# One list of projections for both mixers, dealt out in other shares

## The chip, the cores and the metric

The kernel runs on one core of a Trainium2 chip. Its engines work side by side, each through its own queue in order: TensorE (PE) multiplies matrices, VectorE (DVE), ScalarE (ACT) and GpSimd (POOL) do the elementwise work, and SyncE (SP) issues the DMAs. The metric is the device time of one launch in microseconds (us), lower is better. Loading of a weight into PE is shown as PEld; it can run beside a matmul.

## What is computed

One encoder block on 1024 tokens of width 1024, in float32. An input projection gives everything that two mixers need; a bidirectional gated linear attention (GLA, 4 heads) and a windowed attention with keys shared by groups of heads (8 heads, 2 key heads, blocks of 128, windows of three blocks) run on it; their outputs are gated, merged and projected, and a SwiGLU feed-forward follows.

```python
h = _rms_norm(x, norm_mix_g[l])
proj = h @ w_in[l]
(g_q, g_k, g_v, g_r, g_lr_f, g_lr_b,
 s_q, s_k, s_v, gate_a, gate_b) = jnp.split(proj, split_at, axis=-1)
y_gla = _gla_branch(g_q, g_k, g_v, g_r, ...) @ w_o_gla[l]
y_swa = _swa_branch(s_q, s_k, s_v, ...) @ w_o_swa[l]
merged = jax.nn.sigmoid(gate_a) * y_gla + jax.nn.sigmoid(gate_b) * y_swa
x = x + merged @ w_out[l]
h2 = _rms_norm(x, norm_ffn_g[l])
gu = h2 @ w_ffn_in[l]
ff_gate, ff_up = gu[..., :D_FF], gu[..., D_FF:]
x = x + (jax.nn.silu(ff_gate) * ff_up) @ w_ffn_out[l]
```

In GLA, each head goes through chunks with a state that is carried forward, and once more backward; here a chunk is 128 tokens, so there are 8 chunks a head and 32 in all. The output of a head is normalized per token and multiplied by silu(r). In the attention, queries and keys are normalized and rotated, and a learned logit per head joins the softmax.

## The kernel before

**Precision.** Every float32 matrix product is done in three matmuls in a reduced float32 form: an operand is split into a high part (ACT copies it) and a remainder (POOL or DVE subtracts), and high x high, high x low and low x high add up. A weight unit is a tile of 128x512 (256 KB) that `wunit` (L61 to L68) loads on SP's queue, copies on ACT (`wh`, L65) and subtracts on POOL (`wl`, L67).

**Projections as fillers.** The input projection is cut into named pieces that run as generators, one matmul a step. `proj_f(name, m)` (L161) makes a 128x1024 piece with the features on the partitions: 2 units, 48 matmuls, and then two tiles that DVE scales by the norm (L147) and SP stores to a scratch in DRAM. `proj_t(name, n)` (L180) makes a 1024x512 piece with the tokens on the partitions: 16 units, 192 matmuls, and eight tiles that ACT scales (L208) and SP stores (L209). `next_unit` (L156) takes the weight units in the order in which the pieces were made, up to three ahead. All pieces wait in the list `dense` (L213). `fill(n)` (L215) runs n steps of it, `need(key)` (L224) runs it until a stored piece is there, and `slot(stages, n)` (L228) calls the given stages one after the other and spreads n steps between them.

**GLA.** 32 chunks go through six stages: `g_gates`, `g_sums`, `g_scores`, `g_out`, and in the order of the backward pass `g_back_out` and `g_turn`. The loop at L474 deals them out to slots: chunk n has its gates in slot n, its sums in n + 1, its scores in n + 2, its output in n + 3; the backward output is in slot cb (L468), and the turn, which transposes the normalized output and stores it, one slot later. In a slot the latest stage comes first (the turn, then the backward output, the output, scores, sums, gates). From slot 35 on only backward outputs and turns of the last head are left (the drain). `dense` holds at that time v0, q1, k1, q2, k2, v1, q3, k3, skv, sq0 and sq1, and a slot asks for 64, 48 or 20 steps (L475).

**Attention.** After GLA's pools are closed (L478), those of the attention are opened, and their constants are loaded on SP's queue (L484 to L489). Then r0 to r7 and ga0, gb0 to ga7, gb7 join `dense` (L618 to L620). Sixteen pairs of key group and query block run through `k_prep` and `k_turn` (keys: load, norm, rotation, transpose), `a_prep` and `a_turn` (queries), `a_scores` (four heads, and the softmax behind the last of them, ending in the scaling at L588), `a_probs` (transposes of the probabilities, L599) and `a_out`. `todo` (L621) has 22 slots of 70 steps; what is left of `dense` runs at the end (L637).

**The merge.** Its pools are opened when the attention's are closed (L638). For each half of the tokens, 8 tiles of the GLA output are loaded, gated and split (L664 to L678), 8 tiles of the attention output are loaded and split (L679 to L687), and then groups of 24 matmuls multiply them with the output weights (L652, L695), before the output projection and the feed-forward.

**What sets the order.** PE's instructions of the two loops stand under `tc.manual_schedule` (L473, L633), which keeps PE's order as written within each loop. All else, the order on ACT, DVE, POOL and SP included, comes from a scheduler that goes by dependences, priorities and free buffers. In the trace of before, matmuls of the second loop stand between those of the end of the first.

Of the kernel before, what the change touches and what calls it, by code (L numbers as in the profile page):

```python
# [16 lines left out]
KT = 8  # L17
HT = 512
NH = 4
NC = 8  # L20
# [7 lines left out]
def body(tc, i, out):  # L28
    nc = tc.nc
    with ExitStack() as root:  # L30
# [9 lines left out]
        def nm(s):  # L40
            uid[0] += 1
            return f"{s}_{uid[0]}"

        def mmtile(shape=(P, 512), dt=F32):
            return psm.tile(list(shape), dt, tag="mm", name=nm("mm"))
# [4 lines left out]
        def scratch(name, shape=(P, 512)):  # L50
            return dram.tile(list(shape), F32, tag=name, name=name)

        def stage(shape=(P, 512), dt=F32):
            return stg.tile(list(shape), dt, tag="st", name=nm("st"))
# [15 lines left out]
        def mm(o, a, b, start, stop):  # L70
            nc.tensor.matmul(o, a, b, start=start, stop=stop)  # L71
# [67 lines left out]
        def proj_f_out(name, b):  # L139
            for s in range(2):  # L140
                d = scratch(f"{name}_{s}")
                t = stage()
                if name[0] == "q":
                    nc.vector.scalar_tensor_tensor(t, b[s], 128 ** -0.5, rstd[:, s * HT:(s + 1) * HT],
                                                   op0=ALU.mult, op1=ALU.mult)
                else:
                    nc.vector.tensor_tensor(t, b[s], rstd[:, s * HT:(s + 1) * HT], op=ALU.mult)  # L147
                nc.sync.dma_start(out=d, in_=t)
                scr[name, s] = d
# [6 lines left out]
        def next_unit():  # L156
            while plan and len(ready) <= AHEAD:
                ready.append(wunit(plan.pop(0)))
            return ready.pop(0)

        def proj_f(name, m):  # L161
            plan.extend(i["w_f"][m, u] for u in range(2))

            def steps():
                b = [mmtile(), mmtile()]
                for u in range(2):
                    h, l = next_unit()
                    for kk in range(4):
                        k = u * 4 + kk
                        c = slice(kk * P, (kk + 1) * P)  # L170
                        st, sp = k == 0, k == KT - 1
                        for o, w, x, f0, f1 in ((b[0], h, xh[k][0], st, False), (b[0], h, xl[k][0], False, False),
                                                (b[1], h, xh[k][1], st, False), (b[1], h, xl[k][1], False, False),
                                                (b[0], l, xh[k][0], False, sp), (b[1], l, xh[k][1], False, sp)):
                            mm(o, w[:, c], x, f0, f1)
                            yield
                proj_f_out(name, b)
            return steps()

        def proj_t(name, n):  # L180
            for s in range(2):
                plan.extend(i["w_t"][n, k] for k in range(KT))

            def steps():
                for s in range(2):
                    b = [mmtile() for _ in range(4)]
                    us = []

                    def unit_mm(k, t):
                        h, l = us[k]  # L190
                        c = slice(t * P, (t + 1) * P)
                        st, sp = k == 0, k == KT - 1
                        for x, w, f0, f1 in ((xh, h, st, False), (xh, l, False, False), (xl, h, False, sp)):
                            mm(b[t], x[k][s][:, c], w, f0, f1)
                            yield

                    for k in range(KT):
                        us.append(next_unit())
                        if k < KT - 2:
                            for t in range(4):  # L200
                                yield from unit_mm(k, t)
                    for t in range(4):
                        yield from unit_mm(KT - 2, t)
                        yield from unit_mm(KT - 1, t)
                        ti = s * 4 + t
                        d = scratch(f"{name}_{ti}")
                        o = stage()
                        nc.scalar.activation(o, b[t], AF.Copy, scale=rstdt[:, ti:ti + 1])  # L208
                        nc.sync.dma_start(out=d, in_=o)  # L209
                        scr[name, ti] = d  # L210
            return steps()

        dense = []  # L213

        def fill(n):  # L215

            while n > 0 and dense:
                try:
                    next(dense[0])
                    n -= 1  # L220
                except StopIteration:
                    dense.pop(0)

        def need(key):  # L224
            while key not in scr:
                fill(12)

        def slot(stages, n):  # L228

            stages = [f for f in stages if f]  # L230
            done = 0
            for j, f in enumerate(stages):
                f()
                t = n * (j + 1) // len(stages)
                fill(t - done)
                done = t
# [213 lines left out]
        def g_turn(hd, c):  # L450
# [6 lines left out]
            for j in range(2):  # L457
# [1 line left out]

        dense += [proj_t("v0", 0), proj_f("q1", 2), proj_f("k1", 3), proj_f("q2", 4), proj_f("k2", 5),  # L460
                  proj_t("v1", 1), proj_f("q3", 6), proj_f("k3", 7), proj_t("skv", 2), proj_t("sq0", 3),
                  proj_t("sq1", 4)]

        at = {}
        last = 0
        for n in range(NH * NC):
            hd, c = divmod(n, NC)
            cb = hd * NC + NC + 3 + (NC - 1 - c)  # L468
            for j, (t, f) in enumerate(((n, g_gates), (n + 1, g_sums), (n + 2, g_scores), (n + 3, g_out),
                                        (cb, g_back_out), (cb + 1, g_turn))):  # L470
                at[t, j] = (f, hd, c)
                last = max(last, t)
        with tc.manual_schedule(engines={mybir.EngineType.PE}):  # L473
            for t in range(last + 1):  # L474
                n = 64 if t < 4 else 48 if t < NH * NC + 3 else 20  # L475
                slot([(lambda v=at[t, j]: v[0](*v[1:])) if (t, j) in at else None for j in (5, 4, 3, 2, 1, 0)], n)
        need(("sq0", 7))
        glas.close()  # L478


# [42 lines left out]

        def k_prep(t):
            kv = sw.tile([P, 4, P], F32, tag="kvr", name=nm("kvr"), bufs=1)
            nc.sync.dma_start(out=kv.rearrange("p a b -> p (a b)"), in_=scr["skv", t])
            v2 = kv[:, 2:4].rearrange("p a b -> p (a b)")
            nc.scalar.activation(vSh[t], v2, AF.Copy)
            nc.gpsimd.tensor_tensor(vSl[t], v2, vSh[t].bitcast(F32), op=ALU.subtract)
            keys[t] = norm_rope(kv[:, 0:2], 2, t, kg, 1.0 / 128, EPS, epst)  # L530
# [84 lines left out]
                nc.sync.dma_start(out=scr["b", 4 * g + h, n // 4][:, (n % 4) * P:(n % 4 + 1) * P],  # L615
                                  in_=ob[:, h])

        dense += [proj_f(f"r{m}", 8 + m) for m in range(8)]  # L618
        for m in range(8):
            dense += [proj_f(f"ga{m}", 16 + m), proj_f(f"gb{m}", 24 + m)]  # L620
        todo = [[] for _ in range(2 * KT + 6)]  # L621
        for n in range(2 * KT):
            g, t = divmod(n, KT)
            todo[n + 5].append((a_out, g, t))
            todo[n + 4] += [(a_probs, g, t, kb) for kb in range(3)]
            todo[n + 3] += [(a_scores, g, t, h) for h in range(4)]
            todo[n + 2].append((a_turn, g, t))
            todo[n + 1].append((a_prep, g, t))
            if n < KT:
                todo[n + 1].append((k_turn, n))  # L630
                todo[n].append((k_prep, n))
        order = (a_out, a_probs, a_scores, a_turn, k_turn, k_prep, a_prep)
        with tc.manual_schedule(engines={mybir.EngineType.PE}):  # L633
            for t, v in enumerate(todo):
                v.sort(key=lambda e: order.index(e[0]))
                slot([lambda e=e: e[0](*e[1:]) for e in v], 70)
            fill(1 << 30)  # L637
        swas.close()  # L638
        xstack.close()
# [9 lines left out]
        def btile(tag, dt=F32, bufs=None):  # L649
            return bt.tile([P, HT], dt, tag=tag, name=nm(tag), bufs=bufs)  # L650
# [11 lines left out]
        for s in range(2):  # L662
            oa, ob = ([], []), ([], [])
            for k in range(KT):  # L664
                o = btile("lo")
                nc.sync.dma_start(out=o, in_=scr["o", k, s])
                r = btile("lr")
# [195 lines left out]
```

## Time and profile before

| what | us |
|---|---|
| median of the runs (3) | 1959.8 |
| lowest and highest | 1957.63, 1961.05 |
| the profiled execution, its device time | 1960.35 |
| its span in the trace | 1958.6 |
| PE busy in the span | 1829.8 (93%) |
| PEld busy | 1491.0 (76%) |
| DVE, ACT, POOL busy | 828.7, 716.4, 722.6 |
| mean granted clock of PE | 0.967 |

The times in the text are microseconds from the start of the span. A page of the profile shows the span in 40 equal slices, with the busy share of each engine in tenths; the clock in the same form is the share of full speed that PE was granted. A row of the timeline has the start, the duration, the engine, the line, the operation and what it writes and reads ("mm<-xh,wl" is a matmul into a tile mm from xh and wl), and in brackets the idle time before it with what ended it. Many matmuls have the line of a helper, L71, and are told apart by their tiles: xh and xl are the halves of the normed input, so a matmul with one of these is a step of a projection (features first: mm<-xh,wh and its kin; tokens first: mm<-wh,xh), ob with ident is a turn, U is a sum, vr, vh and vl belong to the values, p with ident is a transpose of probabilities, oah, oal and obh, obl are the merge's operands. Matmuls are pipelined: one starts before the one ahead of it has ended, so their durations add up to more than the time that they take.

### The profile page before, as it was taken

The numbers are of one execution on the slowest core, as the hardware profiler recorded it, in microseconds if no ns is written. First come the engines' busy times: TensorE is split into PE (matmuls) and PEld (weight loads), VectorE is DVE, ScalarE is ACT, GpSimd is POOL, SyncE is SP. The second block draws the span as 40 slices with busy tenths as digits, with TensorE's granted clock in tenths as the row PEclk, the third lists the DMA queues.
The fourth block names the chain that finished last, engine by engine and source line by source line (L and its number), as shares of the span: only waits on it lengthen the run. The fifth ranks groups of instructions, "written<-read, shape, count | busy, mean of one in ns | idle before, by whom it ended". The sixth has DMA issues, their size and how long they took to land. (4 is left out here: it accounts for less than half of the span.)

```text
span 1958.6 us, 24074 instructions
## 1 busy us (share of the span) xinstructions
PE 1829.8 (93%) x8340; PEld 1491.0 (76%) x8340; DVE 828.7 (42%) x1783; ACT 716.4 (37%) x1607; POOL 722.6 (37%) x632
## 2 busy tenths in 40 slices
PE   5899999998389999995798999899999999999999
PEld 3688888887268888873587888688888888888887
DVE  7235566669477766554535234221112111221112
ACT  3344566678433433334444334422112211221120
POOL 6344445544043322221455445533223322332231
PEclk9999999999689999996799999999999999999999
DMA  5343444442233323323557444111121112111212
GB/s 156 95 132 100 132 125 130 138 143 76 60 111 108 97 89 95 103 78 116 170 155 214 144 130 124 38 49 41 44 57 49 42 45 60 49 42 45 60 49 87
DMA packets 126665, 184.91 MB, mean 94 GB/s; under 512 B 14574, under 2 KB 50414, under 8 KB 126544
## 3 DMA queue, kind: packets, MB, share of 16 engines
q1 hardware_dynamic: 126544, 183.38, 31.3%
q8 instruction: 66, 1.08, 0.2%
q14 instruction: 55, 0.45, 0.1%
HBM read 143.48 MB, written 39.85 MB: 94 GB/s over the span
## 5 line engine op out<-in xcount | busy, mean ns | idle before, releaser
L67 POOL TENSOR_TENSOR wl<-wr,wh 128x512 fp32r<-128x512 f32 (+1 forms) x386 | 493.9, 1281 | 923.6 <-ACT wh L65 828.6
L65 ACT ACTIVATE wh<-wr 128x512 fp32r<-128x512 f32 (+1 forms) x386 | 237.3, 615 | 726.9 <-PE mm L71 690.6
L71 PE MATMUL mm<-yh,wh 128*128 128x512 f32 x704 | 276.5, 393 | 0.0
L71 PE MATMUL mm<-yl,wh 128*128 128x512 f32 x704 | 276.0, 392 | 0.0
L71 PE MATMUL mm<-xh,wh 128*128 128x512 f32 (+1 forms) x528 | 213.3, 404 | 14.2 <-ACT xh L277 11.5
L71 PE MATMUL mm<-xl,wh 128*128 128x512 f32 (+1 forms) x528 | 214.2, 406 | 10.4 <-DVE xl L278 10.3
L71 PE MATMUL mm<-yh,wl 128*128 128x512 f32 x704 | 220.5, 390 | 0.0
L71 PE MATMUL mm<-xh,wl 128*128 128x512 f32 (+1 forms) x528 | 178.1, 404 | 0.0
L71 PEld LDWEIGHTS mm<-yh,wh 128*128 128x128 f32 x704 | 132.5, 188 | 33.8 <-DVE st L745 6.7
L71 PEld LDWEIGHTS mm<-yh,wl 128*128 128x128 f32 x704 | 132.7, 189 | 28.4 <-issue 0.8
L71 PEld LDWEIGHTS mm<-yl,wh 128*128 128x128 f32 x704 | 132.6, 188 | 27.8 <-issue 0.8
L71 PE MATMUL mm<-fh,wh 128*128 128x512 f32 x352 | 137.5, 391 | 0.0
L71 PE MATMUL mm<-fl,wh 128*128 128x512 f32 x352 | 137.1, 389 | 0.2 <-DVE fl L749 0.2
L745 DVE TENSOR_TENSOR st<-mm,st 128x512 f32<-128x512 f32 x44 | 30.4, 692 | 244.6 <-PE mm L71 216.4
L71 PEld LDWEIGHTS mm<-xl,wh 128*128 128x128 f32 (+1 forms) x528 | 100.6, 191 | 35.9 <-DVE xl L278 15.9
L71 PE MATMUL mm<-wl,xh 128*128 128x512 f32 x320 | 128.0, 400 | 0.0
L71 PE MATMUL mm<-wh,xh 128*128 128x512 f32 x320 | 127.1, 397 | 0.0
L71 PE MATMUL mm<-wh,xl 128*128 128x512 f32 x320 | 127.0, 397 | 0.0
L71 PEld LDWEIGHTS mm<-xh,wh 128*128 128x128 f32 (+1 forms) x528 | 100.6, 191 | 34.7 <-ACT xh L277 11.5
L71 PEld LDWEIGHTS mm<-xh,wl 128*128 128x128 f32 (+1 forms) x528 | 98.5, 191 | 19.0
L71 PE MATMUL mm<-fh,wl 128*128 128x512 f32 x352 | 109.0, 389 | 0.0
L774 DVE TENSOR_TENSOR x<-mm,x 128x512 f32<-128x512 f32 x48 | 30.9, 686 | 152.8 <-PE mm L71 152.8
(218 smaller groups left out, 3343.2 us busy)
## 6 DMA issues: line engine op xcount, KB each, us to landing
wr<-in_w_fi_dram SPq DMA_DIRECT2D x88, 256.0 KB, 2.6
wr<-in_w_t_dram SPq DMA_DIRECT2D x80, 256.0 KB, 2.7
wr<-in_w_f_dram SPq DMA_DIRECT2D x64, 256.0 KB, 2.8
wr<-in_w_fo_dram SPq DMA_DIRECT2D x48, 192.0 KB, 2.3
wr<-in_w_oa_dram SPq DMA_DIRECT2D x32, 256.0 KB, 2.8
wr<-in_w_ob_dram SPq DMA_DIRECT2D x32, 256.0 KB, 2.7
wr<-in_w_out_dram SPq DMA_DIRECT2D x32, 256.0 KB, 2.9
xr<-in_xT_dram SPq DMA_DIRECT2D x16, 256.0 KB, 2.8
```

What stands on the lines that cost most here:

```text
L65: nc.scalar.activation(h, raw, AF.Copy)
L67: nc.gpsimd.tensor_tensor(l, raw, h.bitcast(F32), op=ALU.subtract)
L71: nc.tensor.matmul(o, a, b, start=start, stop=stop)
L745: nc.vector.tensor_tensor(u, bu[s], g, op=ALU.mult)
L774: nc.vector.tensor_tensor(x1[m][s], y[s], x1[m][s], op=ALU.add)
```

## The change

All pieces go into `dense` before GLA starts, in the same order as before: r0 to r7 and the gates stand behind sq1. The steps per slot are 40 in the first six slots of GLA, 31 up to slot 34 and 18 in the drain; 60 in the first two slots of the attention, 46 in the next sixteen and 28 in the rest. The turn of the last head comes two slots behind its backward output instead of one, so that the loop has one more slot. The wait for the last piece of sq0 behind the loop goes, and `k_prep` has one for its piece of skv.

```diff
         dense += [proj_t("v0", 0), proj_f("q1", 2), proj_f("k1", 3), proj_f("q2", 4), proj_f("k2", 5),
                   proj_t("v1", 1), proj_f("q3", 6), proj_f("k3", 7), proj_t("skv", 2), proj_t("sq0", 3),
-                  proj_t("sq1", 4)]
+                  proj_t("sq1", 4)] + [proj_f(f"r{m}", 8 + m) for m in range(8)]
+        for m in range(8):
+            dense += [proj_f(f"ga{m}", 16 + m), proj_f(f"gb{m}", 24 + m)]
...
             for j, (t, f) in enumerate(((n, g_gates), (n + 1, g_sums), (n + 2, g_scores), (n + 3, g_out),
-                                        (cb, g_back_out), (cb + 1, g_turn))):
+                                        (cb, g_back_out), (cb + (2 if hd == NH - 1 else 1), g_turn))):
...
             for t in range(last + 1):
-                n = 64 if t < 4 else 48 if t < NH * NC + 3 else 20
+                n = 40 if t < 6 else 31 if t < NH * NC + 3 else 18
...
-        need(("sq0", 7))
         glas.close()
...
         def k_prep(t):
             kv = sw.tile([P, 4, P], F32, tag="kvr", name=nm("kvr"), bufs=1)
+            need(("skv", t))
...
-        dense += [proj_f(f"r{m}", 8 + m) for m in range(8)]
-        for m in range(8):
-            dense += [proj_f(f"ga{m}", 16 + m), proj_f(f"gb{m}", 24 + m)]
         todo = [[] for _ in range(2 * KT + 6)]
...
-                slot([lambda e=e: e[0](*e[1:]) for e in v], 70)
+                slot([lambda e=e: e[0](*e[1:]) for e in v], 60 if t < 2 else 46 if t < 2 * KT + 2 else 28)
             fill(1 << 30)
```

## The prediction

> **What bounds the kernel now.** I read the page first, its 40 slices above all, then busy time by stretch, then single rows of the timeline.
>
> ```profile
> span 1958.6 us, 24074 instructions
> ...
> PE   5899999998389999995798999899999999999999
> ...
> PEclk9999999999689999996799999999999999999999
> ```
>
> A slice is 49 us. TensorE (PE) is the bound nearly everywhere, except in two holes, around slices 10 to 12 and 19 to 20, where its clock is lower too. The slots of the diff end in both. Busy time by stretch (the columns are the stretch, its length, then busy us with instruction counts of PE, PEld, DVE, ACT and POOL, then granted clock, DMA share, GB/s):
>
> ```profile
> 72.30:432.60 360.30, 360.29 (x1824) 301.64 (x1824) 193.13 (x442) 203.22 (x519) 168.51 (x161) 1.00 0.43 127
> 432.60:545.60 113.00, 65.06 (x369) 52.56 (x368) 82.13 (x277) 71.49 (x247) 27.33 (x33) 0.78 0.25 73
> 545.60:873.00 327.40, 327.37 (x1556) 270.82 (x1557) 213.55 (x601) 117.41 (x302) 95.15 (x98) 0.99 0.32 98
> 873.00:906.00 33.00, 24.55 (x107) 19.17 (x106) 18.91 (x61) 15.12 (x41) 1.29 (x1) 0.84 0.16 48
> 906.00:972.60 66.60, 38.28 (x120) 25.54 (x120) 31.51 (x33) 27.03 (x45) 24.49 (x19) 0.69 0.57 180
> ```
>
> Filled slots leave PE no idle time at all (row 1, row 3); the holes are rows 2, 4 and 5. From 432.6 us the first list of projections is used up: 256 + 20 x 48 = 1216 steps go to slots 0 to 23, the last 32 to slot 24. Then come the drain of the GLA mixer, the start of the attention, and from 873 us the attention without filling and the start of the merge.
>
> To price a hole I need what a matmul costs when nothing waits, and that is its pitch, not its duration:
>
> ```profile
> 263.53 0.38 PE L454 MATMUL ch<-ident,ob 128*128 128x128 f32 x2
> ...
> 269.25 0.39 PE L71 MATMUL mm<-wh,xl 128*128 128x512 f32 x1
> ...
> 270.89 0.39 PE L71 MATMUL mm<-wh,xh 128*128 128x512 f32 x1
> ...
> 277.97 0.38 PE L454 MATMUL ch<-ident,ob 128*128 128x128 f32 x2
> ```
>
> The middle rows are first and last of 8 steps: 1.64 / 7 = 0.234 us a step, though each is shown with 0.39. From turn to turn a GLA slot takes 14.44 us: 48 steps are 11.2, so the 28 small matmuls of six stages take 3.2 us, 0.116 each.
>
> **The change part by part.** A step is one matmul; proj_f has 48, proj_t 192. The list is now: v0, v1, skv, sq0, sq1 give 960, q1 to k3 six times 48 = 288, together 1248; r, ga, gb give 24 x 48 = 1152; 2400 in all. No matmul is added or removed; each fills another place.
>
> GLA slots. 6 x 40 + 29 x 31 + 10 x 18 = 1319 steps (the last turn moves one slot later, so the loop has 45 slots). The list lasts. A full slot becomes 31 x 0.234 + 3.2 = 10.5 us. Does something else become late in it? The tightest chain goes from the sums to the next slot's scores:
>
> ```profile
> 317.42 0.28 PE L71 MATMUL ch<-U,ll 128*128 128x256 f32 x1
> ...
> 321.37 0.78 POOL L359 TENSOR_TENSOR kl<-en,kh 128x256 fp32r<-128x256 f32 x1
> ```
>
> It needs 322.15 - 317.54 = 4.6 us. The new distance is 10.5 less the sums' own 0.5 and the scores' turn before them (0.7 + 5 steps, 1.2): 8.1 us. Room 3.5. Engine load:
>
> ```profile
> 335.86:350.33 14.47, 14.47 (x77) 12.21 (x76) 11.58 (x29) 11.34 (x33) 6.84 (x7) 1.00 0.47 142
> ```
>
> DVE 11.6 and ACT 11.3 us in one of the fullest slots, with four weight units converted in it (31 steps bring 2.6). Even unshrunk they would exceed 10.5 by 1.1, on 29 slots 32 us; with the projections' share removed (ACT: 1.4 units and some 0.8 output tiles fewer) they fit. I take 0, bounds 0 and 32.
>
> First slots. 40 instead of 64 brings g_out(0,0), the first to use v0, closer to v0's first tile:
>
> ```profile
> 92.95 0.69 ACT L208 ACTIVATE st<-mm,rstdt 128x512 f32<-128x512 f32 x1 [0.41 <-PE mm L71]
> ...
> 100.50 0.74 POOL L370 TENSOR_TENSOR vl<-vr,vh 128x256 fp32r<-128x256 f32 x1 [0.49 <-ACT vh L369]
> ```
>
> From copy through DRAM to the split tile 8.3 us; the tile is done at step 79 and read at step 120, 41 x 0.234 = 9.6 us plus 1.2 of stages. It holds by 2.5 us. All later need() keys are done long before (q1, k1 after 288 steps, needed after 302), so need adds nothing; that of skv is met too, and the removed need(sq0) was met already.
>
> Hole 1, row 2. Its 113.0 us hold 369 matmuls. How many of them are steps shows by their moving tiles (xh, then xl, in 433 to 546 us):
>
> ```profile
> 433.00:546.00 113.00, 15.81 (x47) 0.78 0.25 73
> 433.00:546.00 113.00, 9.56 (x24) 0.78 0.25 73
> ```
>
> 71 steps. That is the first attention slot's share (70): it depends on nothing there and was pulled ahead into the gaps of the GLA slots. 71 x 0.234 + 298 x 0.116 = 51.2 us of work, so **61.8 us** are empty or half-speed. Where they lie:
>
> ```profile
> 524.96 0.66 PE L454 MATMUL ch<-ident,ob 128*128 128x128 f32 x2 [2.68 <-DVE ob L448]
> ...
> 528.94 0.66 PE L454 MATMUL ch<-ident,ob 128*128 128x128 f32 x2 [2.68 <-DVE ob L448]
> ...
> 545.63 0.66 PE L535 MATMUL ch<-ident,qn 128*128 128x128 f32 x2 [16.03 <-DVE qn L515]
> 545.94 1.20 PE L71 MATMUL mm<-xh,wl 128*128 128x512 f32 x2
> ...
> 551.59 0.39 PE L71 MATMUL mm<-xh,wh 128*128 128x512 f32 x1
> ```
>
> A drain slot takes 4.0 us, nearly all the chain to ob. Now it holds 18 steps, 4.2 us, and the turn has two slots: the chain (under 4.0) is hidden. Then the first keys: 545.63 - 528.94 = 16.7 us of copying out, constants, load and norm. Over that now lie 18 steps of the last slot and 60 of the first attention slot: 78 x 0.234 = 18.3 us. The cover is 1.6 us longer than the chain, with SP, ACT and POOL also serving weights; I put 1 us here, bounds 0 and 14 (the 60 steps pulled ahead again). The half-speed matmuls after it go: 14 steps in 5.65 us instead of 3.3, **2.4 us**.
>
> Hole 2a, row 4. A filled attention slot gives the small matmuls' pitch:
>
> ```profile
> 817.10:839.40 22.30, 22.30 (x108) 18.53 (x107) 13.35 (x38) 8.39 (x20) 5.28 (x5) 1.00 0.26 83
> ```
>
> 22.3 - 70 x 0.234 = 5.9 us for 38, 0.155 each. 107 x 0.155 = 16.6 of 33.0 us: **16.4 us** go, as the slots now hold 2 x 60 + 16 x 46 + 3 x 28 = 940 steps (the 22nd slot has no stage and fills nothing) of the 1081 left, and 141 remain for the end.
>
> Hole 2b, row 5. 120 x 0.234 = 28.1 of 66.6 us: **38.5 us** empty or slow, while the merge's operands are made:
>
> ```profile
> 905.79 0.49 PE L71 MATMUL ch<-ph,vSl 128*128 128x512 f32 x1
> ...
> 909.95 0.32 SPq L666 DMA_DIRECT2D lo<-o  x1
> ...
> 941.20 1.36 DVE L676 TENSOR_TENSOR oal<-lo,oah 128x512 fp32r<-128x512 f32 x2
> ...
> 961.67 0.69 DVE L685 TENSOR_TENSOR obl<-lo,obh 128x512 fp32r<-128x512 f32 x1 [1.37 <-ACT obh L684]
> ```
>
> After the attention's last matmul the GLA half is ready 36.8 us later, the other half 56.6 us. Over it now lie 28 + 141 = 169 steps, 39.5 us. Some 17 stay, and PE has two groups of 24 matmuls of the GLA half for them, 11.2 us: I leave 6 us, bounds 0 and 17.
>
> What the shorter attention slots cost. A slot is now 46 x 0.234 + 5.9 = 16.7 us. One chain is tight, from the fourth head's scores to the first transpose of probabilities:
>
> ```profile
> 834.26 0.56 DVE L568 CUSTOM_DVE_ANT_0 p<-ch,band 128x384 f32<-128x384 f32 x1 [1.60 <-PE ch L71]
> ...
> 840.27 1.39 DVE L588 TENSOR_SCALAR p<-p,rd 128x384 f32<-128x384 f32 x4
> ...
> 843.12 0.60 PE L599 MATMUL ch<-ident,p 128*128 128x128 f32 x4
> ...
> 880.42 2.56 PE L599 MATMUL ch<-ident,p 128*128 128x128 f32 x12 [3.12 <-DVE p L588]
> ```
>
> It takes 7.4 us (834.26 to 841.66) and waits for nothing now, as the transpose comes 8.9 us on. In the new slots of 10 stages four shares of 4.6 steps and the turn and out matmuls (2.5) lie between: 6.8 us. So PE waits some 0.6 to 1 us in about 8 such slots, less in the five of 12 stages (6 shares of 3.83 steps, 8.0 us), and about 2 in the last two: 10 us. Bounds: 0 (the unfilled slot at 880.42 has a shorter queue before it) and rival 1.
>
> Sum: 61.8 + 2.4 + 16.4 + 38.5 = 119.1 us can go; 1 + 6 + 10 = 17 come back. The profiled execution took 1960.35 us (span 1958.6, 1.75 around it), 0.55 over the runs' median, which is nothing beside this: 1960.35 - 119.1 + 17 = **1858 us**.
>
> Busy time would size it otherwise: rows 2, 4 and 5 show 47.9 + 8.5 + 28.3 = 84.7 us without a busy PE, and 1960.35 - 84.7 + 17 = 1893. The Trainium skill (Trainium Kernel Development and Optimization, Performance Expectations) calls matmul busy time a bad measure because matmuls are pipelined; the pitch of 0.234 beside the shown 0.39 agrees, and I go by pitch.
>
> **The rivals.** 1: *The attention's chains become the bound.* One instruction takes two lengths:
>
> ```profile
> 90.30 0.42 DVE L351 TENSOR_TENSOR eb<-eb,qk 128x256 f32<-128x256 f32 x1 [0.45 <-ACT eb L349]
> ...
> 318.78 1.37 DVE L351 TENSOR_TENSOR eb<-eb,qk 128x256 f32<-128x256 f32 x1 [0.88 <-ACT eb L349]
> ```
>
> The second runs beside weight splitting on POOL. One or two such hits of 1 us in the 7.4 us chain of 16 slots cost 16 to 32 us: 1874 to 1890. The Trainium skill (GPSIMD Engine Reference, Specifications) states this contention for VectorE instructions with two SBUF inputs; these rows agree. Against it: the slots bring fewer weight units each. 2: *The merge's preparation does not start under the fill*, because its tiles or queue places come free only with the last projection: 39 us back, 1897. For it: the trace shows no case where it could have started earlier. Against: its loads start 4 us after the last attention matmul, behind the store of that result. 3: *The first attention slot's 60 steps are pulled ahead again*: the keys' chain lies open for up to 14 us, 1871. Against: the drain has few gaps left to pull into. 4: **slower**: weights arrive late in the denser mix.
>
> ```profile
> wr<-in_w_t_dram SPq DMA_DIRECT2D x80, 256.0 KB, 2.7
> wr<-in_w_f_dram SPq DMA_DIRECT2D x64, 256.0 KB, 2.8
> ```
>
> 140 of these units (four go before) feed the list. From 0.73 us late per unit on, the gain of 102 is gone; 1 us late gives 1998. Against it: at 48 steps a slot PE waits for none, and 31 ask for fewer. 5: *The change does nothing*, because the emptied time only moves: 1960. Against: 141 steps are left at the end by count.
>
> **How the numbers follow.** Forecast 0.62; rival 1 0.17; 2 0.08; 3 0.08; 4 0.03; 5 0.02. Range 1838 to 1890: below, all of the 17 us and 3 of counting error; above, rivals 1 and 3 and the 32 us of the GLA slots. Left out are 2, 4, 5 and some tail. A difference of 0.2%, 4 us, is what a measurement here can tell. Faster 0.95, same 0.02, slower 0.03.
>
> **What would show it.** Full GLA slots of 10.5 us without PE idle; PE's slices at 9 where 3, 5 and 7 stood, and its clock at 9 with them; no wait of 16 us before the first key transpose; waits of about 1 us on L588 in the later attention slots; the merge's first load some 35 us before the last projection ends. Wrong would be: GLA slots over 11.5 us, waits of 2 us or more in every attention slot, or the merge's loads after the last projection.

## The result and the profile after

The changed kernel takes 1894.28 us (median of 4 runs, 1893.2 to 1898.22) against 1959.62 us (median of four runs, one more than in the table above); the ratio is 0.967, 95% interval 0.965 to 0.969. The forecast was 1858 us, its range 1838 to 1890: the sign and the place of the gain came as forecast, but a third of the forecast gain is missing, and the time lies 4 us outside the range.

The first parts of the page of the changed kernel, to be held against those of before:

```profile
span 1891.4 us, 24031 instructions
...
PE 1820.9 (96%) x8340; PEld 1479.1 (78%) x8340; DVE 848.5 (45%) x1783; ACT 704.1 (37%) x1607; POOL 723.6 (38%) x632
...
PE   5899999999999999998999998999999999999999
...
PEclk9999999999999999998999999999999999999999
```

The 3, 5 and 7 of the holes are gone, and the clock's dips with them. What is missing from the gain can't be seen in tenths: it is spread thinly over slots that show a 9. Busy time by stretch shows it (columns as before). The stretches are the GLA from its first gates to its last turn, the attention from the first transpose of keys to its last matmul, and the merge from the last step of a projection to its 119th matmul, the one that stands at 972.56 us in before:

```profile
72.35:502.46 430.11, 415.75 (x2171) 344.87 (x2172) 291.54 (x698) 260.87 (x753) 192.77 (x190) 0.99 0.40 119
520.96:827.86 306.90, 299.23 (x1432) 241.95 (x1431) 224.71 (x650) 124.49 (x331) 82.37 (x88) 0.99 0.30 92
867.23:906.68 39.45, 33.82 (x121) 24.30 (x120) 17.97 (x22) 16.46 (x28) 20.95 (x15) 0.87 0.56 182
```

Of the loop's 1319 steps 1301 lie in the first stretch, since the last slot's 18 come behind its turn; the other 870 of its 2171 matmuls are small. By the prediction's pitches the bare work (what PE needs when nothing waits) of the three stretches is 1301 x 0.234 + 870 x 0.116 = 405 us, some 290 us (852 steps and 583 small matmuls at 0.155) and 28 us. They take 25, 17 and 11 us more, where the prediction allowed 0, 10 and 6. So the question for the experiments: what holds PE up in full slots, and why three times as long as forecast? PE's waits in the GLA, longest first (engine, tile, line, what it waited for, us in total, times, longest):

```profile
PE ch L71 <- DVE ob L440: 5.0, 6, 1.9
PE ch L71 <- DVE lrS L268: 3.1, 1, 3.1
PE mm L71 <- ACT st L208: 2.7, 2, 2.1
PE ch L71 <- ACT kb L409: 2.7, 7, 0.5
```

The first is not a wait for data. The scores read nothing of L440, which adds the backward output. But they are written to a tile of PSUM, the memory that takes PE's products here, and this tile is the fourth after that output's in a ring of four, so that L440 must have read it first. The second row is the start, as in before. Without it all waits on PE's list for this stretch come to 14 us; the rest of the 25 us shows as busy time of PE (415.75 us for 405). One wait on L440 in the timeline:

```profile
423.06 1.26 POOL L67 TENSOR_TENSOR wl<-wr,wh 128x512 fp32r<-128x512 f32 x1 [0.17 <-ACT wh L65]
423.07 1.40 DVE L333 CAST lh<-e 128x256 fp32r<-128x256 f32 x1
...
424.85 0.41 DVE L440 TENSOR_TENSOR ob<-ob,ch 128x256 f32<-128x256 f32 x1
...
425.41 0.36 PE L71 MATMUL ch<-q,kh 128*128 128x256 f32 x1 [1.85 <-DVE ob L440]
```

POOL starts to split a weight at 423.06; DVE's cast of another tile starts 0.01 us later and ends 0.15 us after POOL. It is not slowed in proportion to its work, it stands until POOL is through: of this line's 32 casts in the GLA seven start while a weight is split, they show 1.25 to 1.40 us, and each ends 0.14 or 0.15 us after the split. Two more stand for 0.70 and 0.88 us beside POOL's shorter splits of q and k (L357, L359); the other 23 take 0.29. L440 is queued behind it, PE behind L440. The Trainium skill (SBUF — State Buffer, Who interferes with whom) states just this: VectorE and GpSimd share a pair of ports as an exclusive lock, held for a whole instruction, and the loser blocks; these rows agree.

Theory A: POOL's weight splitting blocks DVE, whose queue then runs late in every shortened slot. Theory B: DVE's queue has too much work and too many waits in a slot of 10.5 us by itself. Theory A1, beside A: it is the ring of PSUM tiles with L440 in it that turns the lateness into a wait of PE.

### The profile page after: what moved, and what is told of

The parts are those of the page before. It is cut to its first block, busy times and chain, and to the rows that moved or that the text cites. A ratio compares the mean times of both kernels' runs of the same rounds, so it can differ in the third digit from the quotient of the medians.

```text
span 1891.4 us, 24031 instructions
## 1 busy us (share of the span) xinstructions
PE 1820.9 (96%) x8340; PEld 1479.1 (78%) x8340; DVE 848.5 (45%) x1783; ACT 704.1 (37%) x1607; POOL 723.6 (38%) x632
## 5 line engine op out<-in xcount | busy, mean ns | idle before, releaser
L71 PE MATMUL mm<-xh,wh 128*128 128x512 f32 (+1 forms) x528 | 213.6, 405 | 14.4 <-ACT xh L277 11.8
L71 PEld LDWEIGHTS mm<-xl,wh 128*128 128x128 f32 (+1 forms) x528 | 101.0, 191 | 33.3 <-DVE xl L278 14.4
```

## The experiments

All of them change the kernel after, E7 the one before. Times of the stretches, in us, read from the first and last matmuls of each in the timeline; the column "time" is the median of the device times (keys: from the last turn of the GLA to the first transpose of keys):

| run | GLA | keys | attention | merge | time |
|---|---|---|---|---|---|
| before | 456.6 | 16.7 | 360.2 | 66.8 (from the attention's end) | 1959.62 |
| after | 430.1 | 18.5 | 306.9 | 39.4 | 1894.28 |
| E1, no splitting | 405.5 | 18.5 | 294.0 | 35.4 | 1838.41 |
| E2, splitting on DVE | 408.0 | 18.5 | 294.4 | 35.2 | 1845.74 |
| E3, ACT releases | 427.3 | 18.4 | 307.2 | 38.4 | 1890.29 |
| E5, splitting, unused | 430.6 | 18.5 | 305.9 | 38.0 | 1891.12 |
| E8, E2 with 29 and 16 steps | 391.7 | 18.0 | 295.7 | 27.2 | 1840.50 |

### E1: no splitting on POOL

```diff
             nc.scalar.activation(h, raw, AF.Copy)
-            l = wp.tile([P, n], FR, tag="wl", name=nm("wl"), bufs=5)
-            nc.gpsimd.tensor_tensor(l, raw, h.bitcast(F32), op=ALU.subtract)
-            return h, l
+            return h, h
```

> The changed kernel without the splitting of weights on POOL: the high half stands in for the low half, so the low half of the weights is left out of the result; PE has as many matmuls as before, ACT and DVE the same instructions. Theory A (weight splitting on POOL stretches DVE's instructions, L333 1.40 us for 0.29, and so makes the shortened slots late): a full GLA slot goes from 11 to 13 us down to about 10.5, the GLA ends some 20 us earlier (last turn near 482 instead of 502 us), the attention's slots lose 1 us each (16 us), the time falls by 30 to 45 us to 1850 to 1865. Theory B (too much work and too many waits in DVE's queue by itself, POOL or not): GLA slots stay above 11 us, the time falls by less than 10 us.

1838.41 us, 56 us less than the changed kernel: A, and 12 us below the range that A had asked for. GLA lost 24.6 us, the attention 12.9, the merge 4.0; the rest lies ahead of the first gates (6.2 us) and behind the merge.

### E5: splitting put back, unused

E1 takes away the work and the wait for its result at once. This run tells them apart. Its edit, against E1:

```diff
+            l = wp.tile([P, n], FR, tag="wl", name=nm("wl"), bufs=5)
+            nc.gpsimd.tensor_tensor(l, raw, h.bitcast(F32), op=ALU.subtract)
             return h, h
```

> The kernel of e1 with the splitting on POOL put back, but nobody reads its result: PE still takes the high half in place of the low one, which leaves the low half of the weights out. If it is the contention of POOL's work with DVE that costs the time, this is as slow as the changed kernel, 1885 to 1897 us, with the last GLA turn near 500 us. If it is the wait for the low half (1.3 us later on POOL than the high half), this is as fast as e1, 1835 to 1845.

1891.12 us: the whole loss is back though nobody reads the result. The GLA stretch of E1 and then of E5 (after the length stand PE, PEld and DVE):

```profile
66.15:471.64 405.49, 405.49 (x2171) 343.56 (x2172) 231.21 (x698) 269.75 (x753) 71.70 (x96) 1.00 0.42 126
```

```profile
73.23:503.84 430.61, 415.15 (x2172) 343.62 (x2172) 293.40 (x698) 261.28 (x753) 192.45 (x190) 1.00 0.39 119
```

The same 698 instructions keep DVE busy for 231.2 us in one and for 293.4 in the other. These 62 us are standing time, and the GLA is 25 us longer.

A rival would be that POOL's own queue runs late with the splits in it, and that others wait for its tiles. In the changed kernel's GLA PE waits 1.5 us for tiles of POOL (L357 and L359), and DVE for none.

### E2: splitting on DVE

```diff
-            nc.gpsimd.tensor_tensor(l, raw, h.bitcast(F32), op=ALU.subtract)
+            nc.vector.tensor_tensor(l, raw, h.bitcast(F32), op=ALU.subtract)
```

> The changed kernel with the weights split on DVE instead of POOL: 0.69 us of DVE work for each of 386 units, none on POOL. Theory A: 2.6 units a GLA slot cost 1.8 us of DVE but take away some 3 us of stretching, so slots are no longer than before, GLA ends 0 to 15 us earlier, 1880 to 1895 in all. Theory B: slots grow by the added DVE work, 29 x 1.8 = 52 us in GLA and some more in the attention: 1940 or above.

1845.74 us, ratio to before 0.942 (0.941 to 0.944), nothing left out. Theory A had allowed 15 us and gets 48; B is out, for with more work of its own DVE is no longer late. The GLA of E2, and then three groups of instructions over the GLA, first of the changed kernel and then of E2 (busy us, mean ns, idle before):

```profile
69.81:477.83 408.02, 408.02 (x2171) 345.42 (x2172) 289.35 (x791) 268.06 (x753) 75.36 (x96) 0.99 0.42 125
```

```profile
L330 DVE TENSOR_SCALAR e<-e 128x256 f32<-128x256 f32 x32 | 22.9, 714 | 18.0 <-ACT e L329 18.0
L386 DVE COPY_PREDICATED sp<-tri,sp 128x128 f32<-128x128 uint32 x32 | 18.5, 578 | 1.0
L333 DVE CAST lh<-e 128x256 fp32r<-128x256 f32 x32 | 17.6, 549 | 1.1
```

```profile
L333 DVE CAST lh<-e 128x256 fp32r<-128x256 f32 x32 | 11.1, 346 | 1.0
L330 DVE TENSOR_SCALAR e<-e 128x256 f32<-128x256 f32 x32 | 10.1, 317 | 12.4 <-ACT e L329 12.4
L386 DVE COPY_PREDICATED sp<-tri,sp 128x128 f32<-128x128 uint32 x32 | 9.8, 308 | 1.0
```

DVE's busy time is as long as in the changed kernel (289.4 for 291.5 us), with 93 instructions more in it: a split costs DVE 0.70 us itself and had cost it about as much in standing. The difference is that its own work can be placed, and standing falls wherever POOL begins. PE is busy for all of the 408.02 us.

### E3: the backward output leaves PSUM by ACT

```diff
-                nc.vector.tensor_tensor(a.ob, a.ob, o2, op=ALU.add)
+                o2s = gtile("o2s", bufs=2)
+                nc.scalar.copy(o2s, o2)
+                nc.vector.tensor_tensor(a.ob, a.ob, o2s, op=ALU.add)
```

> The changed kernel, where ACT copies the backward output out of PSUM and DVE adds from SBUF. Theory A1 (the scores wait for the PSUM buffer of the backward output, four tiles earlier in a ring of four, whose reader L440 stands late in DVE's queue): the scores' waits on L440 (5.0 us shown, up to 1.9 each) go, the GLA ends 5 to 15 us earlier, 1880 to 1890. Rival (DVE is late for everything, and the next late reader takes its place): the waits move to L409, L407 or L384, the time stays within 4 us of 1894.

1890.29 us, at the edge between both. The waits on L440 are gone, and this stands first in their place:

```profile
PE ch L71 <- ACT kb L409: 8.3, 11, 1.8
```

GLA gains 2.8 us. The ring passes the lateness to PE, but any reader in it does that (kb is the next tile's): A1 names the door, not the cause.

### E4: the last head's turn in the next slot again

```diff
-(cb + (2 if hd == NH - 1 else 1), g_turn)
+(cb + 1, g_turn)
```

> The changed kernel with the last head's turn one slot after its backward output again. If the second slot is what hides the chain to the normalized output (3.6 us against 9 steps, 2.1 us): each of the drain's 8 slots waits 1.5 to 2 us, 12 to 16 us in all, while one slot of 18 steps less in the loop leaves 18 more for the end; 1903 to 1910. If the 18 steps alone were enough: within 4 us of 1894.

1901.34 us, 2 us under the expected range. Turns in the drain wait again, 10.3 us over seven of them, two of which are:

```profile
480.67 0.41 PE L454 MATMUL ch<-ident,ob 128*128 128x128 f32 x2 [2.17 <-DVE ob L448]
...
501.26 0.41 PE L454 MATMUL ch<-ident,ob 128*128 128x128 f32 x2 [2.54 <-DVE ob L448]
```

The GLA is 8.3 us longer with 18 steps (4.2 us) less in it, so the second slot is worth 12.5 us; the merge gives some back for its longer cover. The step of the prediction holds.

### E6: one list, old shares

```diff
-                n = 40 if t < 6 else 31 if t < NH * NC + 3 else 18
+                n = 64 if t < 4 else 48 if t < NH * NC + 3 else 20
...
-                slot([lambda e=e: e[0](*e[1:]) for e in v], 60 if t < 2 else 46 if t < 2 * KT + 2 else 28)
+                slot([lambda e=e: e[0](*e[1:]) for e in v], 70)
```

> The changed kernel with the old steps per slot (64, 48, 20 and 70): one list alone. Steps by count: 256 + 31 x 48 + 10 x 20 = 1944 in GLA, 456 left, gone in the 7th of the 22 attention slots. Theory (time only moves: an emptied slot costs its chain): GLA slots of 14.4 us without waits, drain filled, the first keys covered; then some 11 attention slots of 11.5 us for 5.9 us of work, 60 us, and an open merge, 39 us. 1842 + 99 = 1940, range 1925 to 1955. If one list were what brings the gain: near 1894.

1970.84 us, 1.006 of before (1.004 to 1.008): one list with the old shares brings nothing, it is 0.6% slower than two. The slices of PE:

```profile
PE   6899999999999997675799999899999999999999
```

The GLA's hole is gone, the attention's is twice as long. The steps end at 755.5 us and the attention at 915.3, 159.8 us for 14 slots, 11.4 each; the expectation had counted 11 slots, and had put the open merge at 39 us where it has 40 over its work of 27 (67.3 us). With 14 slots its sum is 1959; 12 us are not accounted for.

### E7: the kernel before, splitting on DVE

The edit of E2.

> The kernel before with the weights split on DVE. Theory (the stretching costs time only where slots are short; filled slots of 14.4 and 22 us have room): the filled stretches to 433 us and from 546 to 873 us keep their lengths, and the time moves by less than 12 us, 1948 to 1960, by the start, the unfilled slots, the merge and the feed-forward. Rival (the split on DVE is worth the same 48 us in any schedule): 1911.

1943.46 us, 15 us less than its reference, 5 under the expected range. But where slots were filled, nothing moved: from the first gates to the last step of the first list it is 359.6 us in both, and the attention takes 360.5 us for 360.2. The gain lies at the start (3.8 us), in the GLA behind the filled slots (2.5), in the merge (4.3) and behind it (6.2). The same standing is there in before, three times in the slot from 306.9 to 321.4 us: L351 at 318.78, which the prediction showed, and these two, which take 0.3 to 0.5 us elsewhere:

```profile
307.76 1.53 DVE L334 TENSOR_TENSOR ll<-e,lh 128x256 fp32r<-128x256 f32 x1
...
310.29 1.23 DVE L430 SCALAR_TENSOR_TENSOR tlb<-kb,decb,thb 128x256 fp32r<-128x256 f32 x1 [0.33 <-ACT thb L429]
```

In slots of 14.4 us it has room. So, by subtraction, 33 of E2's 48 us belong to the shortened slots.

### E9 to E11: how long a slot must be

The changed kernel with 35, 39 and 43 steps in the GLA's slots and 12 in the drain.

```diff
-                n = 40 if t < 6 else 31 if t < NH * NC + 3 else 18
+                n = 40 if t < 6 else 35 if t < NH * NC + 3 else 12
```

> The changed kernel, weights split on POOL as in it, with 35 instead of 31 steps in the GLA slots and 12 instead of 18 in the drain: 56 steps more in GLA, 13.1 us of work, taken from the 141 at the end. A full slot then has 11.4 us. If the slots are late because the stretched queue needs some 11.3 us (10.5 + 0.85 lost), the loss of 24 us nearly goes and GLA from its first gates to its last turn takes 420 to 425 us instead of 430; the merge loses 6 to 9 us of cover; 1888 to 1894. If each slot loses its 0.85 us whatever its length, GLA takes 443 us and the time is 1900 or above.

> As e9, with 39 steps in the GLA slots. Only the GLA stretch is read, from its first gates to its last turn; by bare work it takes 408 + 13.1 + 27.1 = 448 us (408 from e2, 116 steps of 0.234 more than e9). If the loss is a matter of distance between the stages, it shrinks on the way to the 48 steps that lose nothing: 448 to 462. If every slot under 48 loses the same: 471.

> As e9, with 43 steps in the GLA slots. By bare work the GLA stretch takes 475 us. If the loss shrinks with distance: 475 to 482. If every slot under 48 loses the same: 498.

| steps | full slot, bare | steps in the GLA | GLA | bare (408.0 of E2 and the added steps at 0.234) | lost |
|---|---|---|---|---|---|
| 31 | 10.5 | 1301 | 430.1 | 408.0 | 22 |
| 35 | 11.4 | 1363 | 444.4 | 422.5 | 22 |
| 39 | 12.3 | 1479 | 460.2 | 449.7 | 11 |
| 43 | 13.3 | 1595 | 477.2 | 476.8 | 0 |

The expectations counted 56 steps more for 35 a slot; the stretch has 62, since the drain's last slot lies behind the last turn.

E9 (1899.98 us) came out as its rival had it (443 us and 1900): 0.9 us more room a slot saved nothing, and its first wait was

```profile
PE ch L71 <- ACT kb L409: 6.1, 7, 1.8
```

a reader that ACT had late, with 6.1 us for 2.7. A fixed need of 11.3 us a slot, the theory it was to test, is wrong; more steps also bring more units to split. From 39 steps on the loss falls, and at 43 it is gone (the whole kernel took 1918.46 and 1918.78 us in one run each, since the merge had lost its cover). Why 35 loses as much as 31 stays open: the order on DVE and ACT is another one in each of these kernels, and no run holds it fixed.

### E8: E2 with more cover for the merge

```diff
-                n = 40 if t < 6 else 31 if t < NH * NC + 3 else 18
+                n = 40 if t < 6 else 29 if t < NH * NC + 3 else 16
```

> The kernel of e2 with 29 instead of 31 steps in the GLA slots and 16 instead of 18 in the drain: 78 steps more at the end, 18 us more cover for the merge's preparation. If GLA's slots still keep up at 10.0 us: the 8 us between the merge's first 118 matmuls (35.2 us) and their bare work (27) go, 1838 to 1843. If they are at their limit at 10.5 us: GLA loses up to 14 us of what is moved, 1845 to 1855.

1840.50 us, ratio 0.940 (0.939 to 0.942), the fastest complete version here. GLA keeps up at 10 us a slot, and the merge's 119 matmuls take 27.2 us, their bare work: 57.6 us of steps now lie over a preparation of 56.6. Its page:

```profile
span 1837.5 us, 23959 instructions
...
PE 1798.1 (98%) x8340; PEld 1474.1 (80%) x8340; DVE 965.3 (53%) x2169; ACT 709.2 (39%) x1606; POOL 238.7 (13%) x246
```

## Why the prediction was wrong

**What can go: 119.1 us, nearly right.** The forecast without its 17 us of costs was 1841; E8, which pays few of them, takes 1840.5, of which some 10 us are gained outside these stretches, as in E7. So at least some 109 us could be had from the holes, and E8's attention still lies 6 us over its bare 290: the pitch (119) was up to 10 too high, the busy time (84.7) 24 or more too low. The 1893 us that busy time gave is the measured time by chance: its gain and its costs are both too small.

**The drain and the first keys, right.** In the changed kernel no turn of the drain waits, and the first keys come 18.5 us after the last turn, all of it steps:

```profile
498.02 0.38 PE L454 MATMUL ch<-ident,ob 128*128 128x128 f32 x2
...
502.46 0.38 PE L454 MATMUL ch<-ident,ob 128*128 128x128 f32 x2
...
520.96 0.38 PE L537 MATMUL ch<-ident,qn 128*128 128x128 f32 x2
```

The cover of 78 steps, 18.3 us, sufficed: 0 where 1 was set aside, and rival 3 (steps pulled ahead) did not happen.

**"I take 0, bounds 0 and 32" for the GLA slots, wrong: this is the step that failed.** It cost 22 us, by E2's 408.0 as the bare work (25 by the pitches' 405). The sum of DVE's busy time was held against the slot (11.6 us less the projections' share, "they fit"), and the one chain that was followed end to end, from the sums to the scores, nearly kept its room (PE waits 1.5 us for its tiles, at L357 and L359). But a queue in order delays what stands behind a blocked instruction, whatever its chain; L440 was in no chain that I had followed. The row that should have led there stood in the prediction, 1.37 for 0.42 us at L351, but it was priced for the attention alone, in rival 1.

**The attention, mechanism right, too small.** The wait on the probabilities came where it was put:

```profile
PE ch L601 <- DVE p L590: 7.2, 9, 1.6
```

The stretch is 17 us over its bare work where 10 were set aside; E1 leaves 4, and 1.0 us of this wait. So 13 of the 17 are rival 1's blocking (16 to 32 forecast), and the distance alone costs 4 at most.

**The merge, mechanism right, too small.** 11 us for 6; E1 and E2 leave 7, and E8's longer cover takes those. Rival 2 (the preparation waits for the last projection) would have given 1897, near the measured time by chance only, for the loads started 4 us after the attention's last matmul, 35 us ahead of the last step:

```profile
827.86 0.40 PE L71 MATMUL ch<-ph,vSl 128*128 128x512 f32 x1
...
831.96 0.32 SPq L665 DMA_DIRECT2D lo<-o  x1
...
867.23 0.63 PE L71 MATMUL mm<-xh,wl 128*128 128x512 f32 x2
```

**Weights late (rival 4), no.** No wait for a weight is among PE's in the changed kernel. **Nothing changes (rival 5), no;** but E6 is its true form: with the wrong shares the emptied time does move, all of it and 12 us on top.

**Sum.** The three costs came to 22 + 17 + 11 = 50 us instead of 17, 33 of the 36 us between 1858 and 1894. The range failed with the bounds: 32 for the GLA and rival 1's 32 were taken as alternatives, though one cause feeds both.

## What to carry to other kernels

When filler work is spread thinner over slots, the other engines get less time per slot; ask for each queue in order not only whether its sum fits but what stands behind its longest instruction, and which PSUM tile that holds. A DVE instruction that shows two lengths (0.29 and 1.40 us here) is no noise: find what ran beside it, and count it in every stage where the slack goes. Elementwise work given to GpSimd to spare VectorE can cost VectorE as much as it saves; here 0.70 us on DVE was better than 1.28 us on POOL by 48 us in all, and by 15 where the slots had room.

## What the runs showed of the hardware

The blocking does not go by size. A DVE instruction on one column, with two inputs in SBUF (the memory that holds all tiles but those of PSUM), also stood for as long as a split on POOL:

```profile
296.71 1.29 POOL L67 TENSOR_TENSOR wl<-wr,wh 128x512 fp32r<-128x512 f32 x1 [2.79 <-ACT wh L65]
```

```profile
296.76 1.26 DVE L99 TENSOR_TENSOR rt<-rt,rl 128x1 f32<-128x1 f32 x1
```

It takes 0.16 us elsewhere. Instructions with one of their two inputs in PSUM were not held: in the changed kernel's GLA 23 of them (L377, L384, L407, L440) start while a weight is split, and none takes longer than 0.47 us. One such line over the GLA, in the changed kernel and then with no weight split on POOL (E2):

```profile
L440 DVE TENSOR_TENSOR ob<-ob,ch 128x256 f32<-128x256 f32 x28 | 11.6, 415 | 10.8 <-PE ch L71 10.8
```

```profile
L440 DVE TENSOR_TENSOR ob<-ob,ch 128x256 f32<-128x256 f32 x28 | 11.6, 415 | 4.2 <-PE ch L71 4.2
```

With 62 us of standing in the GLA of E5, PE lost 25 us at 10.5 us a slot; at 13.3 us a slot (E11) the loss was under 1.
